# The conditioning's weighted sums on TensorE in column groups, with x loaded ahead of the conditioning weights

## The chip, the cores and the metric

The kernel runs on one NeuronCore of one Trainium2 chip. The metric is the device time of one execution in microseconds (us), lower is better. A core has TensorE (PE, matrix multiplication; its weight loads are listed apart as PEld), VectorE (DVE), ScalarE (ACT), GpSimd (POOL) and SyncE (SP), which in this kernel issues every DMA transfer. Each engine works off its own queue of instructions in order, and semaphores tie the queues together.

## The reference, cut to what matters

One layer of a gated mixer over 2048 tokens of 1024 channels, in fp32:

```python
c_act = jax.nn.silu(c)                                  # (1, 1024)
ada = c_act @ w_ada[l] + b_ada[l]                       # (1, 3072): the conditioning
shift, scale, gate = jnp.split(ada[:, None, :], 3, axis=-1)
h = rms_norm(x, g_pre[l]) * (1.0 + scale) + shift       # (1, 2048, 1024)
(pv, pg, hq, hf, hi, hg, mg_pool, mg_hgrn) = jnp.split(h @ w_in[l], split_idx, axis=-1)
...                                                     # pooling mixer, HGRN2 recurrence, merge
y = merged @ w_out[l]
x = x + gate * rms_norm(y, g_post[l])
```

Every use of `h` needs the shift and the scale of its channel, so nothing of the big input projection can start before the part of `ada` for its 128 channels is there.

## The kernel before

Tokens go in two passes of 1024, each in two halves t of 512 (T). Channels go in eight blocks k of 128. Every fp32 value that goes into the big matmuls is split in two fp32r halves, a high one (a cast on ACT) and a low one (the difference, on DVE); one product then takes three matmuls, high by high, high by low and low by high (`split`, L173, `mm`, L325).

The change concerns the head of the program, the first 70 us or so. There the following is worked through for pass 0 and the first half t = 0:

- **Loads.** SP issues, in this order: small constants, the eight conditioning weight tiles `wa` of quarter q = 0 (`ada_load`, L356: 128 x 512 fp32, 256 KB each, holding 256 shift and 256 scale columns), the eight tiles of x of the first four token blocks (`x_rows`, L458, 256 KB each), two tiles `wre` of `w_in`, and then for q = 1, 2, 3 again eight `wa` and two `wre` (L1152 to L1159). x of the second half t = 1 follows much later, just before the last product group (L1195). Transfers rotate over eight semaphores, so that at most eight are under way.
- **The conditioning.** For each quarter q, `ada_sum` (L368) accumulates on DVE the eight products of a `wa` tile with one value of silu(c) per partition: one `tensor_scalar` (L377) and seven `scalar_tensor_tensor` (L379), into `acc`. `ada_done` (L382) adds over the partitions with four fp32 matmuls of `acc` against a column of ones (L386), which also turns the sums into columns, and three tiny DVE operations (L388 to L390) make `shv` and `scv`, the shift and scale columns of channel blocks 2q and 2q+1.
- **x.** `x_first` (L464) takes for each token block the mean square on ACT (two `Square` instructions with an accumulator, `jx`, L452), the reciprocal root `rst` on POOL (L454, L444), and scales the two halves of x on DVE (L470).
- **h.** `h_in` (L490) transposes x in 128 x 128 blocks on TensorE (`xT`, L498), applies scale and shift on ACT (L500, `h`) and splits it (`hB` on ACT, `lB` on DVE, L174).
- **The first product.** `v_job` (L813) makes `psV`, the value projection `hi`: 12 matmuls of 128 x 512 for each channel block k, three for each of four token blocks, accumulated in four PSUM banks over all eight k. 96 of them make up the first group (t = 0, first 512 columns).

`head_in` (L1170) chains these by hand (`after` adds ordering edges): quarter q+1 is summed on DVE in three portions between the splits of quarter q. Which instruction stands where in each engine's queue is in the end decided by the framework's scheduler, which goes by these edges, by data dependence and by its own estimate of times, that of transfers included. From some 75 us on the program is long streams of matmuls.

Of the kernel before, what the change touches and what calls it, by code (L numbers as in the profile page):

```python
# [8 lines left out]
F32 = mybir.dt.float32  # L9
# [6 lines left out]
AX = mybir.AxisListType  # L16
MUL, ADD, SUB, MAX, MIN = ALU.mult, ALU.add, ALU.subtract, ALU.max, ALU.min

P = 128
# [3 lines left out]
NT = T // P  # L23
NB = T // 32
NPASS = SEQ // 1024
KT = D // P
# [45 lines left out]
def tile_block(ctx: ExitStack, tc: tile.TileContext, x, c, w_ada, b_ada, g_pre, g_post, w_in,  # L72
# [3 lines left out]
    V, A, G, PE, SP = nc.vector, nc.scalar, nc.gpsimd, nc.tensor, nc.sync  # L76
# [4 lines left out]
    cst = ctx.enter_context(tc.tile_pool(name="cst", bufs=1))  # L81
# [11 lines left out]
    def utile(name, dt=F32):  # L93
        return up.tile([P, T], dt, tag="u", name=name)
# [4 lines left out]
    def after(ins):  # L99
        return tc.issue_after(ins.ins) if ins is not None else nullcontext()  # L100
# [16 lines left out]
    ident = cst.tile([P, P], F32, name="ident")  # L117
# [27 lines left out]
    def col(nm, i=None):  # L145
        a, b = idx[nm]
        return vec[:, a:b] if i is None else vec[:, a + i:a + i + 1]

    small = cst.tile([P, 64], F32, name="small")
    lbe, lbr, lbp = small[:, 0:8], small[:, 8:16], small[:, 16:24]  # L150
    lb, oml, cact = small[:, 24:32], small[:, 32:40], small[:, 40:48]
# [171 lines left out]
        return w[:, 0:T], w[:, T:2 * T]  # L323

    def mm(o, l, r, start, stop):  # L325
        PE.matmul(o, lhsT=l, rhs=r, start=start, stop=stop, skip_group_check=True)  # L326

    def three(ps, w, rhs, start, stop):

# [13 lines left out]
    psa = [ph.tile([P, T], F32, tag=f"ph{i}", name=f"psa{i}") for i in range(2)]  # L343
# [6 lines left out]
    shv = cst.tile([P, 8], F32, name="shv")  # L350
    scv = cst.tile([P, 8], F32, name="scv")

    one = cst.tile([P, 1], F32, name="one")
    G.memset(one, 1.0)

    def ada_load(q):  # L356
        parts = []
        for kk in range(KT):
            wa = utile(f"wa{q}_{kk}")
            SP.dma_start(wa.rearrange("p (w n) -> p w n", w=2),  # L360
                         w_ada[kk * P:(kk + 1) * P, 0:2 * D].rearrange("p (w n) -> p w n", w=2)
                         [:, :, q * 256:(q + 1) * 256])
            parts.append(wa)
        return parts

    accs = {}

    def ada_sum(q, k0, k1, prev):  # L368

        if k0 == 0:  # L370
            accs[q] = utile(f"acc{q}")
        acc = accs[q]
        with after(prev):
            for kk in range(k0, k1):
                wa = parts[q][kk]
                if kk == 0:
                    it = V.tensor_scalar(acc, wa, cact[:, 0:1], None, op0=MUL)  # L377
                else:
                    it = V.scalar_tensor_tensor(acc, wa, cact[:, kk:kk + 1], acc, op0=MUL, op1=ADD)  # L379
        return it  # L380

    def ada_done(q):  # L382
        acc = accs.pop(q)
        v = psa[0][:, q * 4:q * 4 + 4]
        for j in range(4):
            it = PE.matmul(v[:, j:j + 1], lhsT=acc[:, j * P:(j + 1) * P], rhs=one, start=True, stop=True)  # L386
        sl = slice(q * 2, q * 2 + 2)
        V.tensor_tensor(shv[:, sl], v[:, 0:2], col("bsh")[:, sl], op=ADD)  # L388
        V.tensor_tensor(scv[:, sl], v[:, 2:4], col("bsc")[:, sl], op=ADD)
        iv = V.scalar_tensor_tensor(scv[:, sl], scv[:, sl], 1.0, col("gpre")[:, sl], op0=ADD, op1=MUL)  # L390
        return it, iv
# [55 lines left out]
    def xsq(tok, xs):  # L447

        s2 = sp.tile([P, 2], F32, tag="xss", name=f"xss{tok}")
        for n in range(2):  # L450
            jx = sp.tile([P, T], BF16, tag="jx", name=f"jx{tok}_{n}", bufs=1)
            A.activation(jx, xs[n], AF.Square, scale=1.0 / 32, accum_out=s2[:, n:n + 1])  # L452
        r = rst[:, tok:tok + 1]
        G.tensor_scalar(r, s2[:, 0:1], s2[:, 1:2], EPS, op0=ADD, op1=ADD)  # L454
        tt(r, r, mh[:, 0:1], op=ALU.pow, e=G)
        return r

    def x_rows(tok, load):  # L458
        xs = [utile(f"x{tok}_{n}") for n in range(2)]
        for n in range(2):  # L460
            load(xs[n], x[tok * P:(tok + 1) * P, n * T:(n + 1) * T])
        return xs

    def x_first(t, cx, xss):  # L464
        for tk in range(NT):
            tok = t * NT + tk
            xs = xss[tk]
            r = xsq(tok, xs)
            for n in range(2):
                it = V.tensor_scalar(xs[n], xs[n], r, None, op0=MUL)  # L470
            cx["x"][t, tk] = xs
        return it
# [17 lines left out]
    def h_in(p, t, k, cx):  # L490

        pt_ = px.tile([P, T], F32, tag="px", name=f"xT{p}_{t}_{k}")
        for tk in range(NT):
            if (t, k // 2) in cx["xc"]:
                src = cx["xc"][t, k // 2][tk // 2][:, tk % 2, (k % 2) * P:(k % 2 + 1) * P]
            else:
                src = cx["x"][t, tk][k // 4][:, (k % 4) * P:(k % 4 + 1) * P]
            PE.transpose(pt_[:, tk * P:(tk + 1) * P], src, ident)  # L498
        h32 = utile(f"h32_{p}_{t}_{k}")
        A.activation(h32, pt_, AF.Identity, bias=shv[:, k:k + 1], scale=scv[:, k:k + 1])  # L500
        cx["h32"][t, k] = h32
        nm = ("B11", "B21", "B12", "B22")[2 * t + k % 2]
        return part(p, nm, k // 2, h32, cx)
# [309 lines left out]
    def v_job(p, t, grp, q, cx, hook=None):  # L813
        if q == 0:
            cx["psV"] = [bank(f"psV{p}_{t}_{grp}_{tk}") for tk in range(NT)]
        pss = cx["psV"]
        it = None

        def mul(k, w, tk):
            hh, hl = cx["mv"][("B11", "B21", "B12", "B22")[2 * t + k % 2], k // 2]  # L820
            xh, xl = hh[:, tk * P:(tk + 1) * P], hl[:, tk * P:(tk + 1) * P]
            mm(pss[tk], xh, w[0], k == 0, False)
            mm(pss[tk], xh, w[1], False, False)
            mm(pss[tk], xl, w[0], False, k == KT - 1)

        if q < 3:
            for k2 in range(2):
                w = take(2 if p == 0 and t == 0 and grp == 0 else LOOK)
                with after(it):
                    for tk in range(NT):  # L830
                        mul(2 * q + k2, w, tk)
                if k2 == 0 and hook is not None:
                    it = hook()
            return
        ws = [take(), take(LOOK - 1)]
        for tk in range(NT):
            for k2 in range(2):
                mul(2 * q + k2, ws[k2], tk)
            vt = utile(f"V{p}_{t}_{grp}_{tk}")
            A.copy(vt, pss[tk])  # L840
            store("Vd", cx["Vd"][:, t * NT + tk, grp * T:(grp + 1) * T], vt)
# [247 lines left out]
    cxs = []  # L1089
    for p in range(NPASS):  # L1090
        cx = {k: {} for k in ("sm", "F", "Q", "G", "V", "pw", "Gd", "Pd", "Sd", "gP", "gG", "a", "mg", "x", "xc", "h32", "m32",
                              "mv", "y", "yss")}
# [56 lines left out]
        if steps:  # L1149
            steps.pop(0)()  # L1150

    parts = {0: ada_load(0)}  # L1152
    xss = [x_rows(tk, SP.dma_start) for tk in range(NT)]
    for q in range(4):
        if q:
            parts[q] = ada_load(q)
        if q < 3:
            for k in (2 * q, 2 * q + 1):
                early["v", 0, k] = raw_load(f"e{k}", (krow(w_in, k, O_I), None))  # L1159
    it = ada_sum(0, 0, KT, None)  # L1160
    with after(it):
        it = ada_done(0)[1]
    with after(it):
        it = x_first(0, cxs[0], xss)
    with after(it):
        prep()
        prep()
    behind = {"v": it}

    def head_in(q):  # L1170
        it, iv = None, behind["v"]
        if q:
            with after(iv):
                it, iv = ada_done(q)
        for n, k in enumerate((2 * q, 2 * q + 1)):
            if q < 3:
                iv = ada_sum(q + 1, 2 * n, 2 * n + 2, iv)
            with after(iv):
                ia, iv = h_in(0, 0, k, cxs[0])
        behind["a"] = ia  # L1180
        behind["v"] = ada_sum(q + 1, 4, KT, iv) if q < 3 else iv
        return it

    for p in range(NPASS):
        cx = cxs[p]

        mixes = [lambda p=p, i=i, cx=cx: h_mix(p, i, cx) for i in range(4)]
        if p == 0:
            head_in(0)
            for q in range(4):  # L1190
                hook = None
                if q < 3:
                    hook = lambda q=q: head_in(q + 1)
                if q == 3:
                    xss = [x_rows(NT + tk, SP.dma_start) for tk in range(NT)]  # L1195
                with after(behind["v"]), after(behind["a"]):
                    v_job(p, 0, 0, q, cx, hook)
            x_first(1, cx, xss)
            const_setup()
            poolw_setup()  # L1200
            late = [lambda k=k: h_in(0, 1, k, cxs[0]) for k in range(KT)]
# [48 lines left out]
        for h in range(NH):  # L1250
            if h + 1 < NH:
                v_head(p, h + 1, cx)
            n = f"{p}_{h}"
# [43 lines left out]
        sums = []  # L1297
# [52 lines left out]
```

## Time and profile before

| | |
|---|---|
| runs | 1811.51, 1814.40, 1814.58 us, median 1814.4 |
| profiled execution, span from first to last instruction | 1814.8 us |
| TensorE busy | 1758.4 us (97%) |
| DVE, ACT, POOL busy | 1184.2, 813.5, 76.8 us |
| TensorE busy in 0 to 20, 20 to 40, 40 to 60, 60 to 80, 80 to 100 us | 3.5, 14.5, 18.2, 17.0, 20.0 us |
| DMA in 10 to 20, 20 to 30, 30 to 40, 40 to 50 us | 383, 387, 390, 72 GB/s |

The records give no other time for the profiled execution than its span, which lies 0.4 us above the median of the three. In the timeline rows that follow, the first number is the start in us from the start of the span, the second the time that the row covers, then engine, line, operation and tiles; `xN` is how many instructions the row merges, and the bracket is how long the engine had been idle and what released it. A plain fp32 matmul has two records, one for each of its passes.

### The profile page before, as it was taken

To read this page: it belongs to the slowest core of one execution; us is meant where nothing else is said; L and a number is where in the kernel's file an instruction comes from. 1 tells how busy PE (TensorE), PEld (TensorE's weight loads), DVE (VectorE), ACT (ScalarE), POOL (GpSimd) and SP (SyncE) were. 2 spreads that over 40 slices of the span, in tenths; PEclk is the share of its full clock that TensorE was granted. 3 is DMA by queue.
4 is the path that set the end of the run, shared out by engine and by line. 5 is a ranking of instruction groups with operands and counts; after the bars stand their busy time and mean duration, and the time that the engine had idled before them with its cause. 6 is when DMAs were issued, how large, how long until landed. Compare 5 with 4: busy or idle time off the path is not lost.

```text
span 1814.8 us, 32278 instructions
## 1 busy us (share of the span) xinstructions
PE 1758.4 (97%) x11957; PEld 1439.5 (79%) x11957; DVE 1184.2 (65%) x2564; ACT 813.5 (45%) x1943; POOL 76.8 (4%) x136
## 2 busy tenths in 40 slices
PE   5899999999999999999999999999999999999997
PEld 4788888888788787888878778888888888788885
DVE  6577898898888984475545165566666565633446
ACT  4655657666566562322332245345344454320032
POOL 1100000000000100000000000000000000000001
PEclk9999999999999999999999999999999999999998
DMA  8548888788878769987986876876865865695367
GB/s 304 188 158 315 283 292 297 282 305 284 284 274 301 260 223 319 340 297 260 327 293 233 285 245 204 277 250 201 286 234 202 281 213 185 220 347 183 128 213 274
DMA packets 272247, 469.40 MB, mean 259 GB/s; under 512 B 20909, under 2 KB 148570, under 8 KB 272090
## 3 DMA queue, kind: packets, MB, share of 16 engines
q1 hardware_dynamic: 272090, 467.35, 74.9%
q8 instruction: 94, 1.54, 0.4%
q14 instruction: 63, 0.52, 0.1%
HBM read 273.80 MB, written 193.46 MB: 257 GB/s over the span
## 4 chain that ended last, share of the span: by engine, by line
PE 59%; DMA 4%; DVE 4%; ACT 1%; issue 1%; POOL 0%; SPq 0%; POOLq 0%; DVEq 0%; ACTq 0%
PE psB L326 10%; PE pafq L326 6%; PE pagp L326 5%; PE pam L326 5%; PE psA L326 5%; PE psy L326 4%; PE pefq L326 3%; PE pegp L326 3%; PE pem L326 2%; PE raV L326 2%; PE psa L326 2%; PE po L326 2%; PE ray L326 2%; PE pbfq L326 2%; PE pbgp L326 1%; PE pbm L326 1%
## 5 line engine op out<-in xcount | busy, mean ns | idle before, releaser
L174 DVE TENSOR_TENSOR whl<-wr,whl 128x512 fp32r<-128x512 f32 x210 | 143.2, 688 | 68.7 <-ACT whl L174 61.3
L174 ACT CAST whl<-wr 128x512 fp32r<-128x512 f32 x210 | 129.5, 620 | 127.7 <-DMA wr<-in_w_hgrn_o_dram 17.9
L326 PE MATMUL psB<-Gh,whl 128*128 128x512 f32 x512 | 158.6, 390 | 0.0
L326 PE MATMUL pagp<-hT,whl 128*128 128x512 f32 x384 | 128.8, 396 | 4.3 <-DVE c22gp L444 2.9
L326 PE MATMUL pam<-hT,whl 128*128 128x512 f32 x384 | 129.7, 399 | 1.4 <-DVE c22m L444 1.3
L326 PE MATMUL pafq<-hT,whl 128*128 128x512 f32 x384 | 126.3, 390 | 0.0
L326 PEld LDWEIGHTS psB<-Gh,whl 128*128 128x128 f32 x512 | 96.1, 188 | 20.4 <-issue 0.5
L630 DVE COPY_PREDICATED PT<-mask,psa 128x256 f32<-128x256 uint8 x160 | 86.2, 549 | 35.9 <-PE psa L326 35.9
L326 PE MATMUL psB<-Gl,whl 128*128 128x512 f32 x256 | 100.0, 391 | 0.0
L326 PEld LDWEIGHTS pagp<-hT,whl 128*128 128x128 f32 x384 | 72.0, 188 | 21.8 <-ACT PV L762 2.5
L326 PE MATMUL psA<-Ph,whl 128*128 128x512 f32 x256 | 83.6, 402 | 3.7 <-DVE sm L444 3.3
L326 PEld LDWEIGHTS pam<-hT,whl 128*128 128x128 f32 x384 | 72.1, 188 | 18.2 <-DVE c22m L444 2.1
L326 PEld LDWEIGHTS pafq<-hT,whl 128*128 128x128 f32 x384 | 72.1, 188 | 15.4 <-ACT c12fq L532 0.4
L326 PE MATMUL psV<-whl,hB 128*128 128x512 f32 x256 | 81.8, 402 | 1.4 <-ACT V L840 1.4
L326 PE MATMUL psy<-whl,mgh 128*128 128x512 f32 x256 | 80.6, 394 | 1.4 <-DMA whl<-scr_y 0.7
L444 DVE TENSOR_TENSOR K<-K,TT 128x256 f32<-128x256 f32 x192 | 80.6, 425 | 1.5 <-PE psa L326 1.4
L326 PE MATMUL pam<-lT,whl 128*128 128x512 f32 x192 | 75.0, 391 | 0.0
L326 PE MATMUL pagp<-lT,whl 128*128 128x512 f32 x192 | 75.0, 390 | 0.0
L326 PE MATMUL pafq<-lT,whl 128*128 128x512 f32 x192 | 74.7, 389 | 0.0
L326 PEld LDWEIGHTS psa<-X,K 128*32 128x32 f32 x2816 | 49.8, 110 | 26.5 <-issue 23.6
L444 DVE TENSOR_TENSOR sm<-psB,sm 128x512 f32<-128x512 f32 x32 | 22.0, 688 | 64.7 <-PE psB L326 63.3
L326 PE MATMUL psa<-X,K 128*32 128x48 f32 (+2 forms) x2816 | 60.7, 208 | 0.0
(455 smaller groups left out, 4441.8 us busy)
## 6 DMA issues: line engine op xcount, KB each, us to landing
wr<-in_w_in_dram SPq DMA_DIRECT2D x122, 256.0 KB
whl<-scr_y SPq DMA_DIRECT2D x44, 512.0 KB
sm<-Sd SPq DMA_DIRECT2D x64, 256.0 KB
scr_v<-rfv SPq DMA_DIRECT2D x56, 256.0 KB
whl<-scr_v SPq DMA_DIRECT2D x28, 512.0 KB
scr_y<-rfy SPq DMA_DIRECT2D x56, 256.0 KB
wa<-in_w_ada_dram SPq DMA_DIRECT2D x32, 256.0 KB
x<-in_x_dram SPq DMA_DIRECT2D x32, 256.0 KB
```

What stands on the lines that cost most here:

```text
L174: return A.copy(hi, src32), (e or V).tensor_tensor(lo, src32, hi.bitcast(F32), op=SUB)
L326: PE.matmul(o, lhsT=l, rhs=r, start=start, stop=stop, skip_group_check=True)
L444: return (e or V).tensor_tensor(o, a, b, op=op)
L630: V.copy_predicated(dst.rearrange("p (c q) a b -> p c q a b", c=NT), m, src.rearrange("p c (a b) -> p c a b", b=b).unsqueeze(2) .broadcast ...
```

## The change

- `ada_sum` and its 32 DVE instructions are gone. `ada_mul` (new) computes a quarter's sums on TensorE: eight matmuls whose stationary operand `cz` is 32 columns wide (silu(c) in column 0, zeros in the other 31) and whose moving operand is a `wa` tile, 512 wide, in plain fp32. Matmul kk writes rows 32(kk % 4) to 32(kk % 4) + 31 of one PSUM bank, so four of them stand in four column groups of the array, and two share a group. ACT copies the bank to SBUF (`ar`).
- `ada_done` transposes `ar` in four 128 x 128 blocks and a DVE reduction adds the four group rows; the three tiny DVE operations follow as before, and the result `iv` still gates `h_in`.
- SP issues x of t = 0 first, then the four quarters of `wa` with their `wre` tiles as before, and right behind the last `wa` all of x of t = 1 (`xs1`), which before was loaded after the first group had almost been done.
- The hooks of `v_job` now fall behind each channel block: `mul_next` (sums of the next quarter) behind k = 0, 1, 3 and `h_pair` (`ada_done` and two `h_in`) behind k = 1, 2, 4.

```diff
+    cz = cst.tile([P, KT, 32], F32, name="cz")
+    G.memset(cz, 0.0)
+    V.tensor_copy(cz[:, :, 0], cact)
+    sums = {}
+
+    def ada_mul(q):
+
+        for kk in range(KT):
+            o = psa[1][32 * (kk % 4):32 * (kk % 4) + 32, :]
+            it = PE.matmul(o, lhsT=cz[:, kk, :], rhs=parts[q][kk], start=kk < 4, stop=kk >= 4, skip_group_check=True)
+        sums[q] = utile(f"ar{q}")
+        A.copy(sums[q], psa[1])
         return it
 
     def ada_done(q):
-        acc = accs.pop(q)
-        v = psa[0][:, q * 4:q * 4 + 4]
+        r = sums.pop(q)
         for j in range(4):
-            it = PE.matmul(v[:, j:j + 1], lhsT=acc[:, j * P:(j + 1) * P], rhs=one, start=True, stop=True)
+            it = PE.transpose(psa[0][:, j * P:(j + 1) * P], r[:, j * P:(j + 1) * P], ident)
+        v = small[:, 56:60]
+        V.tensor_reduce(v, psa[0].rearrange("p (j a b) -> p j a b", j=4, b=32)[:, :, :, 0], axis=AX.X, op=ADD)
...
-    parts = {0: ada_load(0)}
+    parts = {}
     xss = [x_rows(tk, SP.dma_start) for tk in range(NT)]
     for q in range(4):
-        if q:
-            parts[q] = ada_load(q)
+        parts[q] = ada_load(q)
         if q < 3:
             for k in (2 * q, 2 * q + 1):
                 early["v", 0, k] = raw_load(f"e{k}", (krow(w_in, k, O_I), None))
-    it = ada_sum(0, 0, KT, None)
-    with after(it):
-        it = ada_done(0)[1]
-    with after(it):
-        it = x_first(0, cxs[0], xss)
-    with after(it):
+    xs1 = [x_rows(NT + tk, SP.dma_start) for tk in range(NT)]
+    it = ada_mul(0)
+    ix = x_first(0, cxs[0], xss)
+    with after(it), after(ix):
+        it, iv = ada_done(0)
+    with after(iv):
         prep()
         prep()
-    behind = {"v": it}
+    behind = {"pe": it}
...
+    def at_start(k, it):
+
+        behind["pe"] = it
+        if k in (1, 2, 4):
+            it = h_pair((k + 2) // 2)
+        if k in (0, 1, 3):
+            it = mul_next((0, 1, 3).index(k) + 1)
+        return it
...
-                if q == 3:
-                    xss = [x_rows(NT + tk, SP.dma_start) for tk in range(NT)]
                 with after(behind["v"]), after(behind["a"]):
-                    v_job(p, 0, 0, q, cx, hook)
-            x_first(1, cx, xss)
+                    v_job(p, 0, 0, q, cx, at_start)
+            x_first(1, cx, xs1)
```

In ACT's queue, right after the squares of the first half, before the change (`jx3` belongs to token block 3, the last of t = 0; `whl` are splits of the first weights; `h32_0_0_0` is h of channel block 0):

```order
L452 ACTIVATE jx3_1_344,xss3_341<-x3_1_235 128x512
L174 CAST whl0_350<-wre0_238 128x512
L174 CAST whl1_353<-wre1_240 128x512
L500 ACTIVATE h32_0_0_0_364<-xT0_0_0_359,shv_118,scv_119 128x512
L174 CAST hB110_0_366<-h32_0_0_0_364 128x512
```

At the same place after the change (`x4` to `x7` are the four token blocks of t = 1, `ar0` the sums of quarter 0, `psa1` the bank that holds them):

```order
L174 CAST whl1_372<-wre1_241 128x512
L448 ACTIVATE jx4_0_662,xss4_661<-x4_0_299 128x512
L448 ACTIVATE jx4_1_664,xss4_661<-x4_1_300 128x512
L448 ACTIVATE jx5_0_671,xss5_670<-x5_0_303 128x512
L448 ACTIVATE jx5_1_673,xss5_670<-x5_1_304 128x512
L374 COPY ar0_323<-psa1_117 128x512
L448 ACTIVATE jx6_0_680,xss6_679<-x6_0_307 128x512
L448 ACTIVATE jx6_1_682,xss6_679<-x6_1_308 128x512
L448 ACTIVATE jx7_0_689,xss7_688<-x7_0_311 128x512
L448 ACTIVATE jx7_1_691,xss7_688<-x7_1_312 128x512
L496 ACTIVATE h32_0_0_0_380<-xT0_0_0_375,shv_118,scv_119 128x512
L174 CAST hB110_0_382<-h32_0_0_0_380 128x512
```

The eight squares of t = 1, which before stood behind the last h of t = 0, now stand ahead of the first one, four of them ahead of the copy of quarter 0's sums.

In DVE's queue, where the first shift and scale columns are made, before the change (`x0`, `x1` are token blocks of t = 0):

```order
L379 SCALAR_TENSOR_TENSOR acc0_298<-wa0_7_220,small_104,acc0_298 128x512
L388 TENSOR_TENSOR shv_118<-psa0_116,vec_102 128x2
L389 TENSOR_TENSOR scv_119<-psa0_116,vec_102 128x2
L390 SCALAR_TENSOR_TENSOR scv_119<-scv_119,vec_102 128x2
L470 TENSOR_SCALAR x0_0_222<-x0_0_222,rst_147 128x512
```

and after it (`psa0` now holds the transposed sums):

```order
L466 TENSOR_SCALAR x3_1_220<-x3_1_220,rst_148 128x512
L466 TENSOR_SCALAR x4_0_299<-x4_0_299,rst_148 128x512
L466 TENSOR_SCALAR x4_1_300<-x4_1_300,rst_148 128x512
L466 TENSOR_SCALAR x5_0_303<-x5_0_303,rst_148 128x512
L466 TENSOR_SCALAR x5_1_304<-x5_1_304,rst_148 128x512
L382 TENSOR_REDUCE small_104<-psa0_116 128x4
L384 TENSOR_TENSOR shv_118<-small_104,vec_102 128x2
L385 TENSOR_TENSOR scv_119<-small_104,vec_102 128x2
L466 TENSOR_SCALAR x6_0_307<-x6_0_307,rst_148 128x512
L386 SCALAR_TENSOR_TENSOR scv_119<-scv_119,vec_102 128x2
```

The scaling of token blocks 4 and 5 now stands ahead of the reduction, and that of the first half of block 6 between the operations that make the scale columns. On SP the eight transfers of x of t = 1 stand directly behind the eight of the last quarter of `wa`. From the first matmuls of the second half t = 1 on, the queues of all engines hold the same sequence of operations as before.

More of the change, by code (lines that the diff above doesn't have):

```diff
@@ L325, in mm @@
     def mm(o, l, r, start, stop):
-        PE.matmul(o, lhsT=l, rhs=r, start=start, stop=stop, skip_group_check=True)
+        return PE.matmul(o, lhsT=l, rhs=r, start=start, stop=stop, skip_group_check=True)
     def three(ps, w, rhs, start, stop):
@@ L351, in tile_block @@
     scv = cst.tile([P, 8], F32, name="scv")
-    one = cst.tile([P, 1], F32, name="one")
-    G.memset(one, 1.0)
     def ada_load(q):
@@ L364, in ada_load @@
         return parts
[L366 to L379, printed above, removed]
+    cz = cst.tile([P, KT, 32], F32, name="cz")
[8 more added lines that the diff above has]
+        A.copy(sums[q], psa[1])
         return it
     def ada_done(q):
-        acc = accs.pop(q)
-        v = psa[0][:, q * 4:q * 4 + 4]
+        r = sums.pop(q)
         for j in range(4):
-            it = PE.matmul(v[:, j:j + 1], lhsT=acc[:, j * P:(j + 1) * P], rhs=one, start=True, stop=True)
+            it = PE.transpose(psa[0][:, j * P:(j + 1) * P], r[:, j * P:(j + 1) * P], ident)
+        v = small[:, 56:60]
+        V.tensor_reduce(v, psa[0].rearrange("p (j a b) -> p j a b", j=4, b=32)[:, :, :, 0], axis=AX.X, op=ADD)
         sl = slice(q * 2, q * 2 + 2)
@@ L823, in mul @@
             mm(pss[tk], xh, w[1], False, False)
-            mm(pss[tk], xl, w[0], False, k == KT - 1)
+            return mm(pss[tk], xl, w[0], False, k == KT - 1)
         if q < 3:
@@ L830, in v_job @@
                     for tk in range(NT):
-                        mul(2 * q + k2, w, tk)
-                if k2 == 0 and hook is not None:
-                    it = hook()
+                        im = mul(2 * q + k2, w, tk)
+                if hook is not None:
+                    it = hook(2 * q + k2, im)
             return
@@ L1159, in tile_block, with h_pair, mul_next @@
                 early["v", 0, k] = raw_load(f"e{k}", (krow(w_in, k, O_I), None))
-    it = ada_sum(0, 0, KT, None)
-    with after(it):
-        it = ada_done(0)[1]
-    with after(it):
-        it = x_first(0, cxs[0], xss)
-    with after(it):
+    xs1 = [x_rows(NT + tk, SP.dma_start) for tk in range(NT)]
[4 more added lines that the diff above has]
+    with after(iv):
         prep()
         prep()
-    behind = {"v": it}
[L1170 to L1178, printed above, removed]
-                ia, iv = h_in(0, 0, k, cxs[0])
-        behind["a"] = ia
-        behind["v"] = ada_sum(q + 1, 4, KT, iv) if q < 3 else iv
+    behind = {"pe": it}
+    def h_pair(q):
+        with after(behind["pe"]):
+            it, iv = ada_done(q)
+        for k in (2 * q, 2 * q + 1):
+            with after(iv), after(it):
+                ia, iv = h_in(0, 0, k, cxs[0])
+        behind.update(pe=it, a=ia, v=iv)
+        return it
+    def mul_next(q):
+        with after(behind["pe"]):
+            behind["pe"] = ada_mul(q)
+        return behind["pe"]
+    def at_start(k, it):
[4 more added lines that the diff above has]
+            it = mul_next((0, 1, 3).index(k) + 1)
         return it
@@ L1188, in tile_block @@
         if p == 0:
-            head_in(0)
+            for k in range(2):
+                with after(it), after(iv):
+                    ia, iv = h_in(0, 0, k, cxs[0])
+            behind.update(a=ia, v=iv)
             for q in range(4):
-                hook = None
-                if q < 3:
-                    hook = lambda q=q: head_in(q + 1)
-                if q == 3:
-                    xss = [x_rows(NT + tk, SP.dma_start) for tk in range(NT)]
                 with after(behind["v"]), after(behind["a"]):
-                    v_job(p, 0, 0, q, cx, hook)
-            x_first(1, cx, xss)
+                    v_job(p, 0, 0, q, cx, at_start)
+            x_first(1, cx, xs1)
             const_setup()
```

## The prediction

> **What bounds the kernel now.** I read the page first: parts 1 and 2 say which engine and where it has holes.
>
> ```profile
> PE 1758.4 (97%) x11957; PEld 1439.5 (79%) x11957; DVE 1184.2 (65%) x2564; ACT 813.5 (45%) x1943; POOL 76.8 (4%) x136
> PE   5899999999999999999999999999999999999997
> ```
>
> TensorE is the bound nearly everywhere; its one large hole is the first slice (45 us) and some of the second. All that the change touches lies there, so I asked for the waits of TensorE in the first 80 us (total us, times, longest):
>
> ```profile
> PE psa L386 <- DVE acc L379: 14.9, 4, 9.7
> PE xT L498 <- DVE x L470: 5.2, 5, 1.5
> ...
> PE psV L326 <- ACT V L840: 1.4, 1, 1.4
> ```
>
> 14.9 us is TensorE waiting for the sums on DVE: what the change wants to remove. Then TensorE's timeline, for where these waits fall:
>
> ```profile
> 24.32 2.06 PE L326 MATMUL psV<-whl,hB 128*128 128x512 f32 x4
> ...
> 30.67 1.05 PE L386 MATMUL psa<-one,acc 128*128 128x1 f32 x8 [1.99 <-DVE acc L379]
> ...
> 32.14 0.39 PE L326 MATMUL psV<-whl,lB 128*128 128x512 f32 x1
> ...
> 36.91 0.39 PE L326 MATMUL psV<-whl,lB 128*128 128x512 f32 x1
> 37.14 1.03 PE L498 MATMUL xT<-ident,x 128*128 128x128 f32 x8
> 39.56 1.05 PE L386 MATMUL psa<-one,acc 128*128 128x1 f32 x8 [1.39 <-DVE acc L379]
> ...
> 48.93 1.05 PE L386 MATMUL psa<-one,acc 128*128 128x1 f32 x8 [1.81 <-DVE acc L379]
> ...
> 59.49 0.39 PE L326 MATMUL psV<-whl,lB 128*128 128x512 f32 x1
> ...
> 61.52 0.74 PE L326 MATMUL psV<-whl,hB 128*128 128x512 f32 x2 [1.42 <-ACT V L840]
> ...
> 69.47 0.44 PE L498 MATMUL xT<-ident,x 128*128 128x128 f32 x2 [1.49 <-DVE x L470]
> ```
>
> The first 96 psV matmuls run from 24.32 to 59.88 us. Between the two lB rows at 32.14 and 36.91 lie 21 of them: 4.77 / 21 = 0.227 us each when nothing waits, so 96 take 21.8 us. Behind the group two more holes of 1.42 and 1.49 us belong to t = 1 (copies of psV behind late squares on ACT, late scaling of x). From 70 us on TensorE is full and the queues are the same before and after; a delay of the end of this group passes through whole to the end of the program. So the sum is: when does the stream of psV start, and how long does the group take.
>
> **DMA first, since the loads are reordered.** SP's own rows, and ACT's first use of x:
>
> ```profile
> 14.08 1.02 SPq L178 DMA_DIRECT2D wre<-in_w_in_dram  x2
> ...
> 27.33 1.09 SPq L178 DMA_DIRECT2D wre<-in_w_in_dram  x2
> 28.75 5.08 SPq L360 DMA_DIRECT2D wa<-in_w_ada_dram  x8
> 34.15 0.34 SPq L178 DMA_DIRECT2D wr<-in_w_in_dram  x1
> ```
>
> ```profile
> 14.08 0.63 ACT L452 ACTIVATE jx<-x 128x512 bf16<-128x512 f32 x1 [7.18 <-DMA x<-in_x_dram]
> ```
>
> ```profile
> 30.00:40.00 10.00, 7.94 (x44) 6.69 (x44) 8.87 (x16) 3.75 (x6) 0.00 (x0) 1.00 1.08 390
> ```
>
> The first x lands at 14.08, the moment at which the transfer eight places behind it is issued: eight are under way, and an issue marks the landing of the eighth before it. From 27.33 to 34.15 ten transfers of 256 KB are issued, 0.68 us each, with the DMA engines full (390 GB/s). The first wa of quarter 3 was issued at 28.75 and lands at 34.15, the eighth at 34.15 + 7 x 0.68 = 38.9. The change puts the same bytes ahead of that point, in another order, so this holds after it too. The eight x tiles of t = 1 come next: the fourth lands at 38.9 + 4 x 0.68 = 41.6, the eighth at 44.4.
>
> **What the change removes.** 28 + 4 DVE sums:
>
> ```profile
> L379 DVE SCALAR_TENSOR_TENSOR acc<-wa,small,acc 128x512 f32<-128x512 f32 x28 | 21.0, 750 | 1.4 <-DMA wa<-in_w_ada_dram 0.7
> L377 DVE TENSOR_SCALAR acc<-wa,small 128x512 f32<-128x512 f32 x4 | 1.9, 480 | 0.0
> ```
>
> 22.9 us of DVE work, and with it TensorE's waits of 1.99, 1.39 and 1.81 us inside the group. It also brings x of t = 0 in first, hence its squares and scaling go beside the load of wa 0.
>
> **What it moves, and the wait that this adds.** In the order of ACT the four squares of token blocks 4 and 5 stand ahead of the copy of quarter 0's sums (ar0), and those of 6 and 7 ahead of the first h. DVE has the scaling of 4 and 5 ahead of the reduction, and of block 6 in the middle of making scv. Their data lands from 39.5 us on. Both engines work in order; what is queued behind is the whole conditioning chain, and TensorE waits for it with nothing else to do. Before, the same squares stood behind the last h. The durations of the chain:
>
> ```profile
> 17.86 0.63 ACT L452 ACTIVATE jx<-x 128x512 bf16<-128x512 f32 x1
> 18.39 0.19 ACT L452 ACTIVATION_READ_ACCUMULATOR jx<-x 128x1 f32 x1
> 18.61 0.63 ACT L452 ACTIVATE jx<-x 128x512 bf16<-128x512 f32 x1
> ...
> 20.06 0.89 DVE L470 TENSOR_SCALAR x<-x,rst 128x512 f32<-128x512 f32 x2 [0.71 <-POOL rst L444]
> ...
> 32.02 0.16 DVE L390 SCALAR_TENSOR_TENSOR scv<-scv,vec 128x2 f32<-128x2 f32 x1
> ...
> 32.28 0.78 ACT L500 ACTIVATE h<-xT,shv,scv 128x512 f32<-128x512 f32 x1 [5.60 <-DVE scv L390]
> ...
> 33.09 0.62 ACT L174 CAST hB<-h 128x512 fp32r<-128x512 f32 x1
> ```
>
> ```profile
> L840 ACT COPY V<-psV 128x512 f32<-128x512 f32 x4 | 2.0, 588 | 0.0
> ```
>
> A square takes 0.75 us start to start, and from a block's last accumulator read (ends 18.58) to its scaling on DVE (20.06) 1.5 us pass. Step by step: the square of the fourth tile 41.6, its read ends 42.4; copy of ar0 to 43.0 (0.59, as the copy of a psV bank); squares of block 6 to 44.5; of block 7 to 46.0. DVE: block 6's root is there at 44.5 + 1.5 = 46.0, its first half is scaled by 46.5 (0.89 / 2), scv follows at 46.6; h 46.7 to 47.5; hB to 48.1. **The psV stream starts at 48.1 us instead of 24.3.**
>
> **What it adds to TensorE.** Three more rounds of sums (quarters 1 to 3) inside the stream, each eight fp32 matmuls of 512 columns, in two passes each: 16 passes. Nearest rows: a plain fp32 128x512 matmul (the gate's sum), and the recurrence's scores, which stand in four 32-column groups as the new ones do:
>
> ```profile
> L421 PE MATMUL pgate<-gacc,ones x4: 590/590/591, 792.5 to 826.1; 128*128 128x512 f32 x4
> ```
>
> ```profile
> 162.40 0.89 PE L326 MATMUL psa<-QR,K 128*32 128x48 f32 x64
> ...
> 792.53 1.02 PE L421 MATMUL pgate<-gacc,ones 128*128 128x512 f32 x2
> ```
>
> The pair of passes covers 1.02 and one lasts 0.59, so they start 0.43 apart; per column 0.84 ns. One at a time 16 passes take 6.9 us, four abreast 1.7. The scores: 64 passes start within 0.89 - 0.21 = 0.68 us (0.21 is what one lasts), 10.8 ns each; 48 columns by 0.84 would be 40 ns, so 3.7 run abreast. I take 6.9 / 3.7 = 1.9 us a round and keep 1.7 and 6.9 as the ends. [...]
>
> Transposes: 24 of x and 12 of ar behind the start, 0.13 us each (1.03 / 8): 4.6 us. Copy, reduction and h of a quarter (about 0.6, 0.2, 2.0 us) lie behind the x transposes and the next round (1.0 + 1.9 us) or behind 12 psV matmuls (2.7 us): nothing, as these rows cover them; if the covers went, some 2.8 us a quarter.
>
> The clock. After a stretch in which TensorE had little to do it ran at half speed:
>
> ```profile
> 46.80:50.20 3.40, 1.59 (x13) 1.31 (x12) 2.78 (x7) 0.00 (x0) 0.00 (x0) 1.00 0.00 0
> 50.20:53.60 3.40, 3.40 (x10) 2.62 (x9) 1.41 (x4) 2.52 (x4) 0.00 (x0) 0.50 0.72 209
> ```
>
> Busy 1.59 of 3.40 us, then 3.4 us at a granted 0.50, worth 1.7 us. [...] The first psV row (four matmuls in 2.06 us, about 0.5 apart) is such a slow start too. After the change TensorE starts cold at 48.1: between 1.0 us (as at 24.3, where about 2 us were slow) and 2.7; I take 1.9.
>
> **Sum.** 48.1 + 21.8 + 3 x 1.9 + 4.6 + 1.9 = 82.1, and 0.2 for the last matmul's end: 82.3 instead of 59.9, +22.4. The holes of 1.42 and 1.49 go, because x of t = 1 is squared and scaled long before; next in line there is TensorE itself. Net +19.5: 1834.3 against the span of 1814.8, which stands 0.4 above the median of 1814.4: **1834 us**. 0.2% of it (3.6 us) is about what can be told from no change.
>
> **Rivals.**
> - *The head does what the change says* (7%): the squares of t = 1 hold nobody up, because their data comes early. Then quarter 0 lands at 14.08 + 7 x 0.68 = 18.8 (where the last x landed before), the round at half clock takes 3.7, copy, transposes, reduction, adds, h and cast some 3.2: psV starts at 25.7, the group ends at 25.7 + 21.8 + 5.7 + 4.6 + 1.0 = 58.8, a gain of 1.1 and 2.9 from the later holes: about 1811, faster. It decides if the fourth x tile of t = 1 lands before some 22 us. Against it stands its place behind 46 full transfers and the 390 GB/s.
> - *Column groups run one behind the other* (7%): 3 x 5.0 more, 1849. For it: moving tiles of 512 columns, where the scores have 48. Against: the overlap of 3.7.
> - *The clock falls between the streams* (12%): a round, transposes and small waits make 3.5 us without psV, and each is paid with 1.7 us of half clock, as at 50.20: 3 x 1.7 = 5.1, 1839. Against: a full round keeps the whole array busy, and before, holes of 1.99 and 1.39 us cost no clock.
>
> **How the numbers follow.** The forecast's own case has 70%, with a start that can be 1 us earlier, rounds at 1.7, transposes at 0.10 (36 x 0.03 = 1.1 us) and 0.9 less of cold clock: some 4 to 5 us down, 1829; rounds of 2.6, colder clock, a hole at each quarter and at the copies of psV: 6 up, 1840. A remaining 4% is for mishaps on the slower side. The range takes in the clock's case with its own spread and a little of the unknown at the low end: 1827 to 1845. Faster by over 0.2%: half of the first rival, 0.03; same 0.04; slower 0.93.
>
> **What would show it.** Right: the timeline of ACT after the change has a long hole ahead of a square of x of t = 1, released by the DMA of x at about 39 to 40 us; the copy of ar0 starts near 42.5; the first psV matmul near 48; the 16 passes of a round start within about 2 us; no wait of TensorE for ACT's copies of psV. Wrong: psV starting before 30 us (the first rival), rounds near 7 us (the second), a granted clock of 0.5 after each round (the third), or an end of the group near 82 us with the total unchanged, which would mean that the later program has slack that I do not see.

## The result, and the profile after

| | before | after |
|---|---|---|
| median of the runs | 1813.57 us (4 runs, 1811.51 to 1814.58) | 1840.06 us (4 runs, 1838.96 to 1843.65) |
| ratio, 95% interval | | 1.0136 [1.0114, 1.0158] |
| span of the profiled execution | 1814.8 us | 1838.4 us |

The change makes the kernel 26.5 us slower by the medians, 23.6 us by the spans; the forecast was 1834 in a range of 1827 to 1845. The profiled execution took 1840.2 us in all, so 1.8 us lie around its span. Part 1 and the first row of part 2 of the page after:

```profile
PE 1765.4 (96%) x12005; PEld 1439.3 (78%) x12005; DVE 1164.2 (63%) x2537; ACT 816.5 (44%) x1947; POOL 76.7 (4%) x136
PE   1999999999999999999999999999999999999997
```

DVE has lost 20.0 us of work and TensorE has gained only 7.0, and yet TensorE's first slice fell from 5 tenths busy to 1, while the second is full now. The waits of TensorE in the first 80 us (total us, times, longest) name what took the place of the 14.9 us for DVE's sums:

```profile
PE psa L380 <- ACT ar L374: 25.4, 1, 25.4
PE psa L372 <- DMA wa<-in_w_ada_dram: 8.9, 1, 8.9
...
PE psV L326 <- ACT hB L174: 1.8, 1, 1.8
PE psV L326 <- DVE lB L174: 0.6, 1, 0.6
```

One wait of 25.4 us: the round of quarter 0 is long done, and TensorE stands before the transposes of `ar` until ACT has copied the bank. What ACT did meanwhile, in its timeline:

```profile
41.89 0.63 ACT L448 ACTIVATE jx<-x 128x512 bf16<-128x512 f32 x1 [20.90 <-DMA x<-in_x_dram]
...
44.82 0.56 ACT L374 COPY ar<-psa 128x512 f32<-128x512 f32 x1
...
48.54 0.78 ACT L496 ACTIVATE h<-xT,shv,scv 128x512 f32<-128x512 f32 x1 [0.22 <-DVE scv L386]
```

Nothing for 20.90 us: it waits for the first x tile of t = 1, which it needs for a square that stands ahead of the copy. And TensorE's timeline from there:

```profile
45.44 1.12 PE L380 MATMUL psa<-ident,ar 128*128 128x128 f32 x4 [25.39 <-ACT ar L374]
...
50.02 1.43 PE L326 MATMUL psV<-whl,hB 128*128 128x512 f32 x5 [1.76 <-ACT hB L174]
52.04 1.22 PE L326 MATMUL psV<-whl,lB 128*128 128x512 f32 x2 [0.59 <-DVE lB L174]
...
55.29 1.93 PE L372 MATMUL psa<-wa,cz 128*32 128x512 f32 x16
...
84.60 0.39 PE L326 MATMUL psV<-whl,lB 128*128 128x512 f32 x1
...
90.27 1.04 PE L494 MATMUL xT<-ident,x 128*128 128x128 f32 x8
```

The stream of psV starts at 50.02 (forecast 48.1), a round inside it lasts 1.93 (1.9), and its 96th matmul, in the row at 84.60, ends at 85.0 (82.3). Behind it nothing waits any more where before stood holes of 1.42 and 1.49 us. From there to the end of the program both kernels' matmuls can be laid on each other: the change is 21.95 us behind at 93 us, 23.6 at 213 us and 23.6 at the end. In between the distance moves between 23 and 28 us, partly because each of the two traces has one stretch of 3.4 us at half clock of its own there (from 645.7 us after the change, from 715.8 before). At the end nothing is given back.

Why the start is 1.9 us later than forecast stands in SP's rows:

```profile
28.49 1.10 SPq L178 DMA_DIRECT2D wre<-in_w_in_dram  x2
30.00 5.48 SPq L357 DMA_DIRECT2D wa<-in_w_ada_dram  x8
35.88 5.57 SPq L457 DMA_DIRECT2D x<-in_x_dram  x8
41.80 0.33 SPq L178 DMA_DIRECT2D wr<-in_w_in_dram  x1
```

From 28.49 to 35.88 ten transfers of 256 KB are issued, 0.74 us each, where before had 0.68. The windows of 20 to 30 us (busy us of each engine, clock, DMA share, GB/s) have the same in bytes; before:

```profile
20.00:30.00 10.00, 6.51 (x24) 4.70 (x24) 9.04 (x16) 4.43 (x8) 1.40 (x3) 1.00 1.09 387
```

After:

```profile
20.00:30.00 10.00, 0.06 (x1) 0.00 (x0) 0.00 (x0) 0.91 (x2) 0.00 (x0) 0.72 1.09 354
```

387 GB/s against 354, with the DMA engines as full. The means of single packets between 16 and 33 us say it too: 46.1 ns for one of 1 KB before, 50.6 after; 84.0 and 90.6 for one of 2 KB. From 20 to 30 us the other engines do almost nothing (the row above), so it is not contention with them. What differs is where the tiles lie. The constant `one` takes 32 bytes of a partition and `cz` 1024, so every place allocated behind it has moved by 992 bytes: the one of the first tile that is loaded, for one (`wa` before, x after), from byte 200960 of a partition (785 x 256) to 201952 (32 bytes short of 789 x 256).

### The profile page after: what moved, and what is told of

It reads as the page before. It is cut to its first block, busy times and chain, and to the rows that moved or that the text cites. A ratio compares the mean times of both kernels' runs of the same rounds, so it can differ in the third digit from the quotient of the medians.

```text
span 1838.4 us, 32323 instructions
## 1 busy us (share of the span) xinstructions
PE 1765.4 (96%) x12005; PEld 1439.3 (78%) x12005; DVE 1164.2 (63%) x2537; ACT 816.5 (44%) x1947; POOL 76.7 (4%) x136
## 4 chain that ended last, share of the span: by engine, by line
PE 58%; DMA 5%; DVE 3%; issue 1%; ACT 1%; POOL 0%; SPq 0%; POOLq 0%; DVEq 0%; ACTq 0%
PE psB L326 9%; PE pafq L326 6%; PE pam L326 5%; PE pagp L326 5%; PE psy L326 4%; PE psA L326 3%; PE pefq L326 3%; PE pegp L326 3%; PE pem L326 3%; PE psa L326 2%; PE po L326 2%; PE ray L326 2%; PE raV L326 2%; PE pbfq L326 1%; PE pbm L326 1%; PE pbgp L326 1%
## 5 line engine op out<-in xcount | busy, mean ns | idle before, releaser
L326 PEld LDWEIGHTS psa<-X,K 128*32 128x32 f32 x2816 | 49.8, 110 | 26.5 <-issue 23.6
```

The costliest lines, as they stand in the source:

```text
L326: return PE.matmul(o, lhsT=l, rhs=r, start=start, stop=stop, skip_group_check=True)
```

## The experiments

**The theory.** The sums on TensorE cost little, and so do the column groups. The loss is the place of t = 1's squares and scalings: x of t = 1 is loaded early, the scheduler puts its consumers ahead of the first copy of the sums, and ACT and DVE work in order. Rivals: the sums on TensorE themselves are dear (a round, its copy and transposes in each quarter, or groups that run one behind the other). A second theory came up with the result: the tiles' addresses make transfers 10% slower. Each ratio below is to runs of the kernel before that were made along with it; `x_first(1, ...)` is the squaring and scaling of t = 1.

**One: hold the squares.** The change, with t = 1's squares and scalings ordered behind the last block of h of t = 0 (the held version, below).

```diff
-            x_first(1, cx, xs1)
+            with after(behind["v"]), after(behind["a"]):
+                x_first(1, cx, xs1)
```

> The changed kernel with one thing added: the squares and the scaling of x of the second half (token blocks 4 to 7) are ordered behind the last h of the first half; its loads stay early and the sums stay on TensorE. Theory (ACT and DVE wait in order behind squares whose data lands at 41 to 47 us): the copy of the first sums follows the first round at about 20 us, the first psV starts at 24 to 25 us instead of 50.0, the group ends near 59 instead of 84.8, no holes behind it: about 1809.5 us, 0.2% under the kernel before. Rival (the rounds on TensorE, their transposes and the cold clock are what costs): 1830 or more.

Measured: 1819.16 us (11 runs), 1.0028 [1.0019, 1.0037]. 20.9 us of the loss are gone, with all the sums still on TensorE and x still loaded early. psV starts at 24.48:

```profile
24.48 1.20 PE L326 MATMUL psV<-whl,hB 128*128 128x512 f32 x4 [1.37 <-ACT hB L174]
```

So the order of ACT's and DVE's queues was the cause (which of the two weighs more was not tried apart); but 1809.5 was missed by 10. The group ends at 58.7 us (59 expected), so the miss lies behind it. TensorE has a new hole there:

```profile
68.06 1.32 PE L494 MATMUL xT<-ident,x 128*128 128x128 f32 x5 [3.58 <-DVE x L466]
```

and POOL's timeline shows where the scaling of block 7 waited:

```profile
66.02 0.61 POOL L137 CAST mask<-mask_i 128x512 uint8<-128x512 int32 x1 [2.06 <-DMA mask_i<-in_mask_dram]
66.59 0.56 POOL L440 TENSOR_TENSOR rst<-rst,mh 128x1 f32<-128x1 f32 x1
```

A cast of a mask that nobody needs yet stands ahead of block 7's reciprocal root and waits 2.06 us for its own load. The same fault as the change's, in small, on a third engine. In the hole, at 67.0 us, the clock fell, for 6.8 us:

```profile
60.00:67.00 7.00, 4.48 (x22) 3.49 (x20) 3.68 (x7) 3.82 (x11) 3.21 (x6) 1.00 0.95 309
67.00:74.00 7.00, 5.94 (x19) 4.98 (x20) 3.79 (x6) 3.79 (x6) 0.72 (x2) 0.51 0.20 60
```

The hole (3.6 us), what the half clock costs (3.4) and a longer wait at the first `pw`, the pooling mixer's product near 190 us (1.6 instead of 0.2), make 8.4 of the miss.

**Two: the early load without the sums.** The kernel before, its sums on VectorE, with the change's order of loads.

```diff
-    parts = {0: ada_load(0)}
+    parts = {}
     xss = [x_rows(tk, SP.dma_start) for tk in range(NT)]
     for q in range(4):
-        if q:
-            parts[q] = ada_load(q)
+        parts[q] = ada_load(q)
...
+    xs1 = [x_rows(NT + tk, SP.dma_start) for tk in range(NT)]
...
-                if q == 3:
-                    xss = [x_rows(NT + tk, SP.dma_start) for tk in range(NT)]
-            x_first(1, cx, xss)
+            x_first(1, cx, xs1)
```

> Sums on VectorE as before, but the loads in the order of the change (x of the first half first, x of the second half behind the last conditioning weights) and nothing held back. In the queues ACT has all eight squares of the second half ahead of the first h, DVE has the scaling of blocks 4 to 7 mixed into the sums of quarter 0, the first one ahead of all sums. Theory (queue order is the cause, whichever engine sums): sums start only after the first scaling at about 44 us, psV at about 59 us, about 1845 us. Rival (the sums on TensorE are the cause): psV near 24 us, at most 1814 us.

Measured: 1844.39 us (2 runs), 1.0166 [1.0141, 1.0191]. The loads alone, with none of the sums moved, make the whole loss and 4 us more, as expected. ACT's square, DVE's first sum, which stands behind the scaling of block 4, and TensorE's wait:

```profile
39.02 0.63 ACT L452 ACTIVATE jx<-x 128x512 bf16<-128x512 f32 x1 [19.11 <-DMA x<-in_x_dram]
```

```profile
41.57 0.88 DVE L470 TENSOR_SCALAR x<-x,rst 128x512 f32<-128x512 f32 x2 [33.62 <-POOL rst L444]
42.37 0.48 DVE L377 TENSOR_SCALAR acc<-wa,small 128x512 f32<-128x512 f32 x1
```

```profile
PE psa L386 <- DVE acc L379: 48.0, 3, 46.1
```

**Three: the sums without the early load.** The change, with x of t = 1 loaded where it was before.

```diff
-    xs1 = [x_rows(NT + tk, SP.dma_start) for tk in range(NT)]
...
+                if q == 3:
+                    xs1 = [x_rows(NT + tk, SP.dma_start) for tk in range(NT)]
```

> The change without its second edit: the sums run on TensorE in four column groups, and block 4 to 7's x is loaded where the kernel before loads it, behind the first group of v; nothing is held by hand (addresses as in the change, 992 bytes on). The copies of the sums stand ahead of block 4's squares on ScalarE again. Theory (the early load of x alone, with the squares that the scheduler pulls ahead behind it, makes the change's loss): the stream of psV starts at 24.5 us as in the held version, and the time is 1816 to 1822, with the packets as slow as in the change. Rival (the sums on TensorE cost most of the loss, each round by more than its 1.9 us): over 1830.

Measured: 1813.72 us (10 runs), 1.0000 [0.9989, 1.0010]: no difference from before, 2 to 8 us better than expected. The stream starts at 24.12, though the packets are as slow as in the change (50.6 ns for 1 KB), and once the first weights are there TensorE's waits up to 80 us are small:

```profile
PE psa L380 <- ACT ar L374: 1.5, 1, 1.5
PE psV L326 <- ACT hB L174: 1.4, 1, 1.4
PE xT L494 <- DVE x L466: 1.0, 2, 0.7
```

In this trace TensorE is 4.3 us ahead of before at 63 us; 1.6 of it is lost at the first `pw` near 187 us. The change's edits are thus told apart: the sums on TensorE, and x of t = 0 ahead of them, cost nothing that these runs show; the early load of x of t = 1, with the squares and scalings that the scheduler pulls ahead behind it, costs everything.

**Four: one column group.** The held version with all eight matmuls of a round in the same 32 columns (copy, transposes and reduction are cut to one group too).

```diff
-            o = psa[1][32 * (kk % 4):32 * (kk % 4) + 32, :]
-            it = PE.matmul(o, lhsT=cz[:, kk, :], rhs=parts[q][kk], start=kk < 4, stop=kk >= 4, skip_group_check=True)
+            o = psa[1][0:32, :]
+            it = PE.matmul(o, lhsT=cz[:, kk, :], rhs=parts[q][kk], start=kk == 0, stop=kk == KT - 1, skip_group_check=True)
```

> The held version (sums on TensorE, squares of the second half behind the last h), with all eight matmuls of a round in one column group of 32 instead of four, and the transposes and the sum over groups cut to one group. Theory (four column groups run side by side): a round inside the stream takes about 6.9 us instead of 1.9, three rounds cost 15 us more than in the held version, about 1824.5 us. Rival (something else than the array sets a round, such as the read of the moving tiles): a round stays near 2 us and the time within 2 us of the held version.

Measured: 1832.00 us (4 runs), 1.0102 [1.0082, 1.0123], 7.5 over the 1824.5 expected, which was reckoned from a held version at 1809.5, and 12.8 over the held version by the medians and 19.4 by the spans; in the head its matmuls run 14.1 us behind the held version's. A round in one group, and in four (held version):

```profile
28.08 7.05 PE L372 MATMUL psa<-wa,cz 128*32 128x512 f32 x16
```

```profile
27.44 1.92 PE L372 MATMUL psa<-wa,cz 128*32 128x512 f32 x16
```

7.05 against 1.92: 3.7 of four groups run side by side, as the recurrence's scores had suggested, and three rounds at 5.13 more would be 15.4. The second rival falls by this.

**Five: addresses, from both sides.** The change with one more 32-byte tile, so that everything behind it is moved by 1024 bytes instead of 992:

```diff
+    pad = cst.tile([P, 8], F32, name="pad")
+    G.memset(pad, 0.0)
     cz = cst.tile([P, KT, 32], F32, name="cz")
```

> The change itself with one more 32-byte tile ahead of cz, so that all tiles behind it lie at the address of before plus 1024 bytes; the order on every queue is the change's. Theory (addresses): pace 0.67 to 0.68, block 7's x lands at about 41.6 to 42 us instead of 43 to 44 and the stream of psV starts at 48 instead of 50.0 us, the hole at the first pw is 0.3 instead of 1.8; together 3 to 3.5 us under the change: 1836.5 to 1837. Rival: pace 0.74, start 50.0, time 1840.

And the kernel before with the same tile behind `one`, which moves everything by 32 bytes and does nothing else:

```diff
     G.memset(one, 1.0)
+    pad = cst.tile([P, 8], F32, name="pad")
+    G.memset(pad, 0.0)
```

> The kernel before with one more 32-byte tile behind the constant one, so that every tile behind it moves by 32 bytes; nothing else is changed. Theory (addresses): pace 0.74 us for 256 KB instead of 0.67, 1 KB packets at 50.6 ns instead of 46.1, the hole at the first pw 1.5 us instead of 0.2, and a time 1.3 to 3 us over the kernel before: 1815 to 1816.6. Rival (the transfers are slowed by TensorE's sums, not by addresses): pace 0.67 and 1813.6.

Measured: the aligned change 1835.05 us (4 runs), 1.0117 [1.0102, 1.0133], 5.0 us under the change (3 to 3.5 expected); the shifted kernel before 1816.28 us (11 runs), 1.0018 [1.0008, 1.0028], 2.7 us over before. The window of 20 to 30 us of the aligned change:

```profile
20.00:30.00 10.00, 0.00 (x0) 0.00 (x0) 0.00 (x0) 0.00 (x0) 0.00 (x0) 0.56 1.08 386
```

and of the shifted kernel before:

```profile
20.00:30.00 10.00, 7.77 (x24) 5.64 (x24) 9.11 (x16) 3.99 (x7) 1.19 (x2) 1.00 1.09 354
```

386 GB/s with the tiles moved by 1024 bytes and TensorE idle beside the loads, 354 with them moved by 32 and TensorE busy for 7.77 of 10 us; before and after the change it was 387 with TensorE at 6.51 and 354 at 0.06. The 1 KB packets take 46.0 and 50.6 ns. The rival, TensorE's reading of the weights, is out: no sum is on TensorE in the shifted kernel. In the aligned change psV starts at 47.0 instead of 50.0, and TensorE's wait at the first `pw` is 0.4 instead of 1.8 us. In the shifted kernel before that wait rose only to 0.6, not to the 1.5 expected. There psV starts no later than before (23.96 us), and what the trace shows of the loss up to the group's end (61.15 instead of 59.88) is the clock, which stands at half for 6.8 us where before it did for 3.4:

```profile
45.75:49.16 3.41, 1.61 (x13) 1.27 (x12) 3.27 (x5) 0.00 (x0) 0.00 (x0) 1.00 0.00 0
49.16:52.57 3.41, 3.41 (x12) 2.83 (x12) 1.04 (x5) 1.57 (x3) 0.00 (x0) 0.50 0.44 114
52.57:55.99 3.42, 3.42 (x10) 2.65 (x9) 2.48 (x5) 2.85 (x6) 0.00 (x0) 0.50 0.89 236
```

So the addresses are shown to change the time of a packet (50.6 ns instead of 46.1 for 1 KB); that slower packets alone make the 2.7 us is not shown.

**Six: two more moves.** The kernel before, moved by 64 and by 128 bytes (the pad 16 and 32 columns wide instead of 8).

> The kernel before with everything behind the constant one moved by 64 bytes instead of 32 (a 64-byte tile). One look, for the size of the grid: if 64 bytes is the grid, 1 KB packets take 46 ns and 256 KB land every 0.67 us as in before; if the grid is 128 or 256 bytes, 50.6 ns and 0.74 us as with 32 bytes (or something between).

> The kernel before with everything behind the constant one moved by 128 bytes. One look: on a grid of 64 or 128 bytes the packets take 46 ns and 256 KB land every 0.67 us, on one of 256 bytes they are as slow as with 32 bytes, 50.6 ns and 0.74 us.

Measured, one run each: 1814.71 and 1812.38 us, which tells nothing of the time, but the same window is plain, moved by 64 bytes:

```profile
20.00:30.00 10.00, 7.71 (x24) 5.58 (x24) 9.11 (x16) 3.83 (x6) 1.06 (x2) 1.00 1.09 354
```

and by 128:

```profile
20.00:30.00 10.00, 6.66 (x24) 4.79 (x24) 9.11 (x16) 3.83 (x7) 1.00 (x2) 1.00 1.10 353
```

As slow as with 32 (50.7 and 50.9 ns for 1 KB). I had thought of a grid of 64 bytes; that fell. Of the moves tried, 0 and 1024 bytes are fast, 32, 64, 128 and 992 are slow. In the kernel before the loaded tiles begin at odd multiples of 256, as the one at 785 x 256; so all the fast places are multiples of 256 and none of the slow ones is. Other moves were not tried, so that every multiple of 256 is fast, or nothing but these, is not shown. All fourteen traces agree: 46.0 to 46.1 ns for 1 KB in the seven with moves of 0 or 1024, 50.6 to 50.9 in the other seven. What the slow places cost does not go by how far a tile was moved: the packets take 4.5 to 4.8 ns more at 1 KB and 4.8 to 6.6 at 2 KB. Why they do is not shown.

**Seven: the held version on aligned addresses,** the first experiment with the tile of the fifth.

> The held version (the change, with block 4 to 7's squares and scales of x ordered behind block 0 and 1's inputs) with one more 32-byte tile ahead of cz, so that every tile behind it lies at the address of before plus 1024 bytes instead of plus 992. Theory (the change's 992 bytes put the destinations of all the transfers off the 64-byte grid, and each packet takes 10% longer for that): 256 KB of the conditioning's weights land every 0.67 to 0.68 us instead of 0.74, the mean of a 1 KB packet is about 46 ns instead of 50.6, the hole at the first pw (1.56 us) falls to about 0.3, and the time falls from 1819.2 by 1.3 to 3 us: 1816 to 1818. Rival (the change's transfers are slower because of what else runs beside them, TensorE's reads of the weights among it): pace 0.74, hole 1.5, time 1819.

Measured: 1813.17 us (11 runs), 0.9995 [0.9985, 1.0005], 6.0 under the held version where 1.3 to 3 were expected. The hole at the first `pw`, which was to go, stayed: 1.7 us. By the two traces 4.1 us are gained: the group ends 2.1 earlier, and 1.7 come from the clock, which stands at half for 3.4 instead of 6.8 us at the late x transposes (these wait 3.15 us now).

**Eight: and the mask casts behind block 7's root.**

```diff
-        tt(r, r, mh[:, 0:1], op=ALU.pow, e=G)
+        last["r"] = tt(r, r, mh[:, 0:1], op=ALU.pow, e=G)
...
-            const_setup()
+            with after(last["r"]):
+                const_setup()
```

> As the held version on aligned addresses, and the three mask casts on GpSimd are ordered behind block 7's rst. In the held version one cast waits 2.06 us for its transfer ahead of block 7's power, the last x transposes start 3.58 us late for it, and the clock stands at half for 6.83 us behind that hole. Theory: the hole falls to about 1.5 us (2.06 less), the second half-speed window goes with it or is cut to 3.4 us (1.7 to 3.4 us less): 3 to 5 us under the aligned held version, 1811 to 1814, no slower than the kernel before. Rival (another input, block 7's x or the squares on ScalarE behind the copies of the sums, is as late): hole 2.5 to 3.5 us, time within 1 us of the aligned held version.

Measured: 1809.81 us (7 runs), 0.9977 [0.9967, 0.9988]: 3.4 under the aligned held version (3 to 5 expected), and faster than both kernels, than the one before by 0.2%. The x transposes wait 1.33 us (1.5 expected), and the stretch in which the clock had fallen is at full speed:

```profile
63.37 0.76 PE L496 MATMUL xT<-ident,x 128*128 128x128 f32 x5 [1.33 <-DVE x L468]
```

```profile
60.00:67.00 7.00, 5.67 (x31) 4.38 (x30) 5.42 (x9) 4.71 (x10) 3.63 (x6) 1.00 0.80 258
67.00:74.00 7.00, 6.95 (x38) 5.59 (x37) 3.70 (x6) 5.35 (x9) 0.00 (x0) 1.00 0.30 84
```

**Nine: are the sums on TensorE worth it then?** The same two holds with the sums on VectorE, first without and then with the masks moved (x of t = 1 loaded behind the last `wa`, held as in the first experiment, the masks as in the eighth). x of t = 0 stays behind the first `wa` here, as in the kernel before, so they differ from the eighth in this too and not in the sums alone.

> The kernel before, sums on VectorE, with one thing taken from the change: x of the second half is loaded right behind the last conditioning weights, its squares and scaling held behind the last h of the first half. Theory: the first group is as before (psV from 24.3 us), and the two holes of 1.42 and 1.49 us behind it go: about 1810.7 us. Rival (the early load collides with the loads of w_in): 1813.6 or more.

> The kernel before (sums on VectorE) with block 4 to 7's x loaded behind the last conditioning weights, their squares and scales held behind block 0 and 1's inputs, and the mask casts behind block 7's rst: the partner of the aligned held version with the masks moved (1809.8), which differs from it in the sums alone. If the sums on TensorE are worth something once the order is mended, this is slower than 1809.8 by more than 0.1%; without that, 1809 to 1811. Theory: the sums' waits of before on VectorE (13.1 us in all with the held order) are outside the steady stream only for the first sum; the three rounds on TensorE cost 3 x 1.9 us there, and the VectorE version has 3 us of waits on the later sums in their place: within 2 us of each other, 1810 to 1812.

Measured: 1811.29 us (11 runs; 1810.7 expected), 0.9988 [0.9976, 1.0001], and 1812.34 us (11 runs), 0.9986 [0.9974, 0.9998]. Against 0.9977 [0.9967, 0.9988] of the eighth the intervals overlap, so these runs don't tell whether sums on TensorE or on VectorE are better once the order is mended. Moving the masks brought nothing here.

## Why the prediction was right, and where its sizes were off

- **The mechanism** (in-order ACT and DVE queues in which squares of t = 1 stand ahead of the first sums' copy): right, and shown from both sides. The hold takes 20.9 us of the loss away, and the loads alone, without the sums, lose 30.
- **The DMA term**: mis-sized. I took 0.68 us a transfer from before, "this holds after it too", with the fourth x tile of t = 1 at 41.6. It was 0.74, because `cz` moved the tiles by 992 bytes (50.6 ns instead of 46.1 for 1 KB); the first x landed at about 41.8 (39.6 in the forecast's count) and psV started at 50.0, not 48.1. On aligned addresses x lands at 38.9 and psV starts at 47.0, 1.1 earlier than my sum, which set the landing 0.7 and the chain behind it 0.4 too late. So the addresses cost 3.0 us, and that 1.1 of them was covered by other errors is luck.
- **The group**: 34.2 us were forecast from the start to its end, 35.0 came: 3 rounds of 1.93 (1.9), and the clock at 0.50 once, from 51.8 to 55.2. The 0.8 is a balance: a wait of 0.59 for `lB` that I had not seen and psV matmuls that came 0.24 apart at full clock where I took 0.227 (1.2 us over 84 of them), against transposes that took 3.9 us inside the stream instead of 4.6.
- **The later holes**: 2.9 us to go, 3.1 went (85.0 - 59.9 = 25.1 at the group's end, 21.95 behind it).
- **"A delay of the end of this group passes through whole"**: at the end of the program so it did, and 1.65 us came on top at the first `pw` near 213 us, where DVE waits for a weight tile that lands late. In the change the aligned addresses take this away; in the aligned held version it stays at 1.7 us, and in the shifted kernel before it is 0.6, so addresses alone don't explain it. What else sets it was not tried.
- **The span**: I set 1814.8 against the median as if it were a time. With the 1.8 us around it, it stands for some 1816.6. The forecast's 1834.3 plus 1.8, and 1.9 + 0.8 - 0.25 + 1.65 of the points above, make 1840.2, the time of the profiled execution.
- **The range**: its low terms (1, 3 x 0.2, 1.1 and 0.9) add up to 3.6 us, not to 4 to 5, so this case's low end was 1831 rather than 1829. The result lies on the other side. No run shows the high end's rounds of 2.6 us; the three rounds of the stream took 1.93.
- **The rivals**: the first (squares hold nobody up, 1811) is what the eighth experiment shows at 1809.8, once somebody orders it so; its condition, early data, was not met. The second is out by the 7.05 against 1.92. The third, a clock that falls behind each round, is out: in the change the clock stands at full (1.00) through the three rounds of the stream. It was at half through the wait, from 24.5 to 48.4 us, and fell once more in the head, behind a window in which TensorE was busy for 1.43 of 3.41 us:

```profile
48.38:51.79 3.41, 1.43 (x5) 0.86 (x5) 2.96 (x7) 3.19 (x5) 1.96 (x2) 1.00 0.44 144
51.79:55.21 3.42, 3.17 (x7) 2.15 (x7) 1.40 (x3) 0.03 (x1) 0.00 (x0) 0.50 0.28 80
```

## What to carry to other kernels

Loading something earlier can also move its consumers earlier in the in-order queues of the other engines, where the scheduler places them, and if the data is not there by then, everything behind them waits (here 20.90 us on ACT); order such consumers by hand behind the chain that the bottleneck engine needs, small ones on GpSimd included (2.06 us there). When a change adds or drops a small constant, look where the big tiles behind it begin now and how long the packets of their loads take: here moves of 32, 64, 128 and 992 bytes took a 1 KB packet from 46.1 to between 50.6 and 50.9 ns, one of 1024 did not. A duration taken from the profile before holds only as long as what it depends on, addresses included, stays as it was (0.68 us a transfer became 0.74).

## What the runs showed of the hardware that I had not expected

- Packets into SBUF tiles moved by 32, 64, 128 or 992 bytes from where they lie in the kernel before, at multiples of 256, took about 10% longer: 50.6 to 50.9 ns instead of 46.1 for 1 KB, and 353 to 354 GB/s instead of 387. With 1024 bytes they took 46.0 ns at 386 GB/s. By the medians the kernel before is 2.7 us slower with its tiles moved by 32 bytes, and the change 5.0 faster with them moved by 1024 instead of 992.
- Four column groups with fp32 operands of 512 moving columns ran 3.7 abreast: 1.92 us for 16 passes against 7.05 in one group.
- In the change the clock stood at 1.00 in a window in which TensorE was busy for 1.43 of 3.41 us, and at 0.50 for the next 3.42 us. In the shifted kernel before TensorE was busy for all of 49.16 to 52.57 us at 0.50, and the 3.42 us behind that were at 0.50 too.
